# A two-layer encoder trunk: the memory norm's weights moved from the rows into the split, and the first transfers reordered

## The chip, the core and the metric

The kernel runs on one core of one Trainium2 chip. The metric is the device time of one execution in microseconds, the median of the runs. Engines: PE (TensorE, matrix products and transposes), DVE (VectorE), ACT (ScalarE), POOL (GpSimd) and SP (SyncE, which only issues transfers here). Each engine works through its own instructions in order and waits on semaphores for the others. Sixteen DMA engines move data between the chip's main memory and the on-chip buffer; matrix products go to a second on-chip memory, PSUM.

## The reference

Two layers of an encoder on 512 tokens of width 1024. Each layer normalizes x, projects it to queries, keys, values and a gate, attends over the tokens (dilated windows in layer 0, grouped queries in layer 1), attends over 256 memory tokens, gates, and projects back. The part that the change touches is the memory branch of layer 0:

```python
def rmsnorm(x, g):
    xf = x.astype(jnp.float32)
    y = xf * lax.rsqrt(jnp.mean(xf * xf, axis=-1, keepdims=True) + EPS)
    return (y * g.astype(jnp.float32)).astype(x.dtype)
...
    for i in range(DEPTH):
        h = rmsnorm(x, norm_g[i])
        mem_h = rmsnorm(mem, mem_norm_g[i])
...
    kv = jnp.einsum('bnd,de->bne', mem_h, w_kv).reshape(Bn, N, 2, MEM_HEADS, HEAD_DIM)
    k = rmsnorm(kv[:, :, 0], kn_g)
    v = kv[:, :, 1]
```

The norm's factor per row, rsqrt of the mean square, is applied later, to the keys' norm and to the values. What has to be in the memory rows before the product is the weight per column, mem_norm_g.

## The kernel before

Every float32 product is made of three matmuls on operands that are split in two: a high part rounded to float32r, and a low part, the rest. ACT makes the high part of a weight piece (line 323), DVE the low part (line 333). A group of matmuls has first the products that need only the high part of the weight (lines 176 and 177), then those with its low part (line 180). Weight pieces are 128x1024 float32, 512 KB, called W0, W1 and so on here in the order of their use.

The program is written out slot by slot by a small driver at build time. After each group of matmuls `W.advance` emits the next work on weights (low parts, high parts, loads) and `drv.tick` lets waiting generators take a step. Every engine then runs its instructions in the order in which they were emitted, whatever is ready.

The beginning goes as follows.

- Lines 1053 to 1075: the first transfers on SP's queue. The norm's weights for the memory as one row, the first half of memory rows 0 to 127, W0 and W1, rows 128 to 255 whole, the second half of rows 0 to 127, W2 and W3, x's norm weights broadcast to 128 partitions (`row_load`), W4 and W5, a small table, and the four 512 KB blocks of x with W6 and W7 between the second and the third.
- Lines 1115 to 1121: PE spreads the row of weights over 128 partitions by matmuls of a row of ones with it (`spread`).
- Lines 1128 to 1148: `times` multiplies a half of the memory rows (128x512) by that on DVE; `turn4` transposes it in four 128x128 pieces on PE; `place_m` splits the result into high and low parts of 128x512. `square` and `factor` make the norm's factor per row on ACT and POOL.
- Line 1189: the product for keys and values, `mem_kv`. The keys, K, take four groups: (u, b) is half u of the contraction with memory rows of block b. W0 and W1 serve u = 0, W2 and W3 u = 1. The values, V, follow with W4 to W7. `ahead(u, b)`, called within a group between its high and low matmuls, emits the splits of the blocks to come: `place_m(1, 0)` in group (0, 0), `place_m(0, 1)` and `place_m(1, 1)` in group (0, 1).
- Lines 1077 to 1095 and 1177: `prep`, which normalizes and transposes x, starts at slot 2 (PD), which is the tick after group (0, 1). In the tick after group (0, 1) it emits the squares of x's first block, x0, on ACT and its factor on POOL; in that after (1, 0) the squares of x1 and the multiplication of x0 on DVE (line 534); in that after (1, 1) the squares of x2, the multiplication of x1 and the transposes of x0 on PE (line 540); in that after V's first group those of x1.
- `W.advance` after group (0, 1) emits the high parts of W4 and W5, that after (1, 0) their low parts, that after (1, 1) the high parts of W6 and W7.

Of the kernel before, what the change touches and what calls it, by code (L numbers as in the profile page):

```python
# [10 lines left out]
F32 = mybir.dt.float32  # L11
F32R = mybir.dt.float32r
AF = mybir.ActivationFunctionType
ALU = mybir.AluOpType
# [14 lines left out]
DIRECT, DIRECT_B = (7,), (3, 4, 5, 6, 7)  # L29
LO_K, TURN_K, HI_V, LO_V = (4, 4), (8, 6), (1, 6), (9, 2)  # L30
PD = 2
EO = 2, 2, 1, 2, 2, 1
YB = {"m": (2, 2), "k": (1, 1, 1), 0: (1, 2, 1), 1: (1, 2, 1)}
Y = [3, 2, 2, 2, 3, 2, 2, 1, 1, 1]
# [9 lines left out]
KEEP_C = {0: 14, 3: 14, 4: 12}  # L44
KEEP = {"T2": 8, "T2b": 6, "O1": 6, "W1": 9, "W2": 10, "W2s": 9, "W1bs": 9, "W2c": 9, "W1b": 7, "W2b": 9, "W1o": 7}
# [86 lines left out]
def trunk_kernel(ctx: ExitStack, tc: tile.TileContext, x, mem, wall, norm_g, mem_norm_g, gcol,  # L132
                 qn_a, kn_a, qn_b, kn_b, ident_d, mask_d, tab_a, tab_b, out):
    nc = tc.nc
    V, A, G, T = nc.vector, nc.scalar, nc.gpsimd, nc.tensor

    pool = ctx.enter_context(tc.tile_pool(name="pool", bufs=1))
# [18 lines left out]
    def at(name="at"):  # L156
        return psum.tile([128, 512], F32, tag="at", name=name, bufs=4)
# [38 lines left out]
    class Weights:  # L196
# [63 lines left out]
            else:  # L260
                queue.dma_start(t, wall[d], **how)  # L261

        def dma(self, most=9):
            while self.allocs and self.live < KEEP_C.get(self.allocs[0][0][0], KEEP[self.allocs[0][2]]) and most:
                most -= 1
                key, d, _ = self.allocs.pop(0)
                self.live += 1
                self.tile[key] = m4(name="wl")
                self.load_at[key] = self.g
                if key[1][0] != "T":  # L270
                    self.at[key] = self.g
                self.load(nc.sync, self.tile[key], d)

        def ripe(self, at, key, force, n=None):
            return key in at and (force or self.g - at[key] >= (LEAD if n is None else n))
# [1 line left out]
        def sum(self, force=False, want=None):  # L277
# [33 lines left out]
                return True  # L311
            return False

        def hi(self, force=False):
            i = self.n_hi
            if i >= len(self.items) or not self.ripe(self.at, self.items[i], force, 1 if self.items[i][1] == "T1" and self.items[i][0] < T1_DMA else None):
                return False
            if i >= RING and self.last[i - RING] > self.g - (not force and self.items[i - RING][1] != "P"):
                return False
            self.n_hi += 1  # L320
            wh = pool.tile([128, 1024], F32R, tag="wh", name="wh", bufs=RING)
            wo = pool.tile([128, 1024], F32R, tag="wo", name="wo", bufs=RING)
            A.copy(wh, self.tile[self.items[i]])  # L323
            self.hi_at.append(self.g)
            self.op.append((wh, wo))
            return True

        def lo(self):
            i = self.n_lo
            self.n_lo += 1  # L330
            wh, wo = self.op[i]
            key = self.items[i]
            V.tensor_tensor(wo, self.tile[key], wh.bitcast(F32), ALU.subtract)  # L333
            self.lo_at[key] = self.g
            self.use(key)

# [30 lines left out]
    W = Weights()  # L367
# [129 lines left out]
    ropeA = tabs[:, 512:2048].rearrange("p (c b s e) -> p c b s e", c=2, b=4, s=6)  # L497
    half = pool.tile([128, 8], F32, name="half")
    rm = pool.tile([128, 6], F32, name="rm")
    ones = tabs[0:1, 0:128]  # L500
    V.memset(half, -0.5)
    V.memset(ones, 1.0)
    A.activation(small.tile([128, 1], F32, tag="sm1", name="warm"), half[:, 0:1], AF.Exp)

    class Act:
# [30 lines left out]
    def turn4(src, hi, lo, mid=None):  # L536

        p = at("xT")
        for k in range(4):
            T.transpose(p[:, k * 128:(k + 1) * 128], src[:, k * 128:(k + 1) * 128], ident)  # L540
# [513 lines left out]
    xt = [m4(name="x") for _ in range(4)]  # L1054
    rows = {}
    mt = [m4(name="m") for _ in range(2)]
    nc.scalar.dma_start(ident, ident_d)
    row0 = m4(name="row0")[0:1, :]
    nc.sync.dma_start(row0, mem_norm_g[0:1, :])
    nc.sync.dma_start(mt[0][:, 0:512], mem[0:128, 0:512])  # L1060
    W.dma(2)
    nc.sync.dma_start(mt[1], mem[128:256])
    nc.sync.dma_start(mt[0][:, 512:1024], mem[0:128, 512:1024])
    W.dma(2)
    row_load("x", norm_g[0:1, :])
    W.dma(2)
    tabA = s2(name="tabA")[:, 0:256].rearrange("p (b c d) -> p b c d", b=2, c=4)
    grA = s2(name="grA")[:, 0:192].rearrange("p (s c) -> p s c", s=6)
    nc.sync.dma_start(gc, gcol)
    for c in range(4):  # L1070
        nc.sync.dma_start(xt[c], xv[c])
        if c % 2 and c < 3:
            W.dma(2)
    H, H2 = {}, {}
    xb = [halves(t) for t in xt]
# [36 lines left out]
                            grA[:, None].to_broadcast([128, 4, 6, 32]), ALU.mult)  # L1112
            yield 1

    row = [at("row") for _ in range(2)]

    def spread(j, *cols):

        for c in cols:
            cs = slice(256 * c, 256 * c + 256)  # L1120
            T.matmul(row[j][:, cs], ones, row0[:, 512 * j + 256 * c:512 * j + 256 * c + 256], start=True, stop=True, skip_group_check=True)

    spread(0, 0, 1)
    mb, M = [halves(t) for t in mt], Act(NM)
    ss = [sm(2, "ss") for _ in range(2)]
    mg = {}

    def times(b, j):

        t = mg[b, j] = s2(name="mg")  # L1130
        V.tensor_tensor(t, mb[b][j], row[j], ALU.mult)

    def square(b, j):

        A.activation(s2(name="sq"), mb[b][j], AF.Square, scale=1.0 / 32.0, accum_out=ss[b][:, j:j + 1])

    def factor(b):

        e = sm(1, "mse")
        G.tensor_tensor(e, ss[b][:, 0:1], ss[b][:, 1:2], ALU.add)  # L1140
        r = rstd_of(e, 1)
        for k, by in enumerate((1.0, QS, 0.5)):
            G.tensor_scalar(rm[:, 2 * k + b:2 * k + b + 1], r, by, None, ALU.mult)

    def place_m(b, j, act=True, p=None):

        cs = slice(b * 128, (b + 1) * 128)
        split(M.block(0, j, cs), M.block(1, j, cs), p or turn4(mg[b, j], None, None), act)

    square(0, 0)  # L1150
    times(0, 0)
    spread(1, 0)
    p = turn4(mg[0, 0], None, None)
    spread(1, 1)
    W.hi(True)
    place_m(0, 0, False, p)
    W.hi(True)
    W.lo()
    times(1, 0)
    W.lo()  # L1160
    for b, j in ((1, 0), (0, 1), (1, 1)):
        square(b, j)
    for b in range(2):
        times(b, 1)
        factor(b)

    def ahead(u, b):

        if (u, b) == (0, 0):
            place_m(1, 0)  # L1170
            W.hi(True)
            W.hi(True)
        if (u, b) == (0, 1):
            place_m(0, 1)
            place_m(1, 1)

    drv.spawn(prep(), PD)
    drv.spawn(setup(), SET_AT)
# [611 lines left out]
```

## Time and profile before

| | us |
|---|---|
| median of 3 runs | 943.32 (943.01 to 944.55) |
| span of the profiled execution | 940.4 |
| PE busy | 932.0 |
| DVE busy | 799.6 |
| ACT busy | 691.6 |
| POOL busy | 348.4 |

The profiled execution is known by its span, from the first to the last instruction. Busy time is the time in which an engine works on an instruction; matmuls are pipelined, so a busy PE need not be at its peak. Rows of a timeline have start, duration, engine, line, operation, what is written from what, the count, and in brackets the idle time before with what ended it. Several instructions of one kind in a row are one row. SPq is SP's queue of transfers, whose rows are the issue, not the transfer. The mean granted clock of PE is 1.000.

### The profile page before, as it was taken

The page shows a single profiled execution, that of the slowest core. Times are in us where ns is not written, and L with a number is a line of the kernel's source. Part 1 is how long each engine was busy: PE and PEld are TensorE (multiplying, and loading weights), DVE is VectorE, ACT ScalarE, POOL GpSimd, SP SyncE. Part 2 cuts the span into 40 slices and gives each one's busy share as a digit, 9 for nine tenths or more (in the row PEclk, how much of TensorE's full clock was granted, in tenths as well). Part 3 has the DMA queues.
Part 4 walks back from the last instruction along what each step waited for, and adds up shares of the span by engine and source line. Part 5 has one row for each costly group of instructions (what it writes and reads, how often), then busy time and mean ns, then how long its engine had stood idle before and what let it go on. Part 6 is the DMA issues. An engine that isn't in the chain of part 4 may idle for free.

```text
span 940.4 us, 16301 instructions
## 1 busy us (share of the span) xinstructions
PE 932.0 (99%) x5500; PEld 819.4 (87%) x5500; DVE 799.6 (85%) x1443; ACT 691.6 (74%) x1720; POOL 348.4 (37%) x494
## 2 busy tenths in 40 slices
PE   8999999999999999999999999999999999999998
PEld 6889888888888888888889998888988999999886
DVE  6998776879888888889788999877998998689978
ACT  7775788677768686867675768537878887789773
POOL 3412425455554545463836111214252440110122
PEclk9999999999999999999999999999999999999999
DMA  9999937869787878696867979979985686785777
GB/s 346 387 259 324 316 93 189 278 133 262 155 251 146 261 155 267 158 268 136 242 177 190 269 202 249 291 239 317 270 201 118 171 240 167 198 225 121 200 159 179
DMA packets 89285, 207.15 MB, mean 220 GB/s; under 512 B 25201, under 2 KB 34417, under 8 KB 89202
## 3 DMA queue, kind: packets, MB, share of 16 engines
q1 hardware_dynamic: 68674, 140.51, 43.5%
q0 software_dynamic: 19520, 63.97, 36.8%
q10 hardware_dynamic: 1008, 1.64, 0.5%
q8 instruction: 43, 0.70, 0.3%
q14 instruction: 40, 0.33, 0.1%
HBM read 158.31 MB, written 11.08 MB: 180 GB/s over the span
## 4 chain that ended last, share of the span: by engine, by line
PE 95%; DVE 2%; ACT 1%; DMA 1%; issue 0%; SPq 0%; DVEq 0%; ACTq 0%
PE pj L177 25%; PE pj L176 25%; PE pj L180 25%; PE qT L645 3%; PE sa L1305 2%; PE oo L1413 2%; PE pt L1392 1%; PE ptb L1619 1%; PE sa L1301 1%; PE xT L540 1%; PE ob L180 1%; PE ob L177 1%; PE ob L176 1%; PE sb L171 1%; PE sb L170 1%; PE sb L172 1%
## 5 line engine op out<-in xcount | busy, mean ns | idle before, releaser
L333 DVE TENSOR_TENSOR wo<-wl,wh 128x1024 fp32r<-128x1024 f32 x258 | 316.3, 1232 | 6.9 <-ACT wh L323 6.7
L323 ACT CAST wh<-wl 128x1024 fp32r<-128x1024 f32 x258 | 272.1, 1061 | 31.0 <-PE pj L177 17.4
L176 PE MATMUL pj<-wh,hS 128*128 128x512 f32 (+1 forms) x416 | 154.4, 380 | 0.0
L177 PE MATMUL pj<-wh,hS 128*128 128x512 f32 (+1 forms) x416 | 149.0, 367 | 0.0
L176 PE MATMUL pj<-wh,h 128*128 128x512 f32 (+1 forms) x312 | 115.3, 378 | 0.0
L177 PE MATMUL pj<-wh,h 128*128 128x512 f32 (+1 forms) x312 | 111.7, 367 | 0.0
L488 POOL TENSOR_TENSOR rstd<-mse,half 128x4 f32<-128x4 f32 (+2 forms) x98 | 103.4, 1056 | 8.2
L180 PE MATMUL pj<-wo,hS 128*128 128x512 f32 (+1 forms) x416 | 99.5, 366 | 0.0
L177 PEld LDWEIGHTS pj<-wh,hS 128*128 128x128 f32 x416 | 78.7, 189 | 11.2
L176 PEld LDWEIGHTS pj<-wh,hS 128*128 128x128 f32 x416 | 78.6, 189 | 11.1 <-DVE sn L420 0.2
L487 POOL TENSOR_SCALAR mse<-hss 128x4 f32<-128x4 f32 (+1 forms) x88 | 47.8, 543 | 101.9 <-ACT junk L633 94.2
L180 PEld LDWEIGHTS pj<-wo,hS 128*128 128x128 f32 x416 | 72.5, 189 | 13.1
L633 ACT ACTIVATE junk<-sn 128x128 f32<-128x128 f32 x264 | 79.4, 311 | 2.7 <-DVE sn L411 2.6
L398 ACT COPY sn<-pj 128x512 f32<-128x512 f32 x122 | 67.1, 588 | 17.8 <-PE pj L180 17.0
L1249 POOL TENSOR_TENSOR ta<-sn,tabs 128x128 f32<-128x128 f32 (+1 forms) x64 | 35.8, 566 | 119.0 <-DVE sn L638 91.8
L180 PE MATMUL pj<-wo,h 128*128 128x512 f32 (+1 forms) x312 | 74.5, 365 | 0.0
L307 POOL DMA_DIRECT2D wl<-wl x34 | 30.2, 897 | 113.3 <-DVE wo L333 73.3
L261 POOL DMA_DIRECT2D wl<-in_wall_dram x40 | 38.0, 966 | 80.4 <-DMA wl<-in_wall_dram 41.0
L177 PEld LDWEIGHTS pj<-wh,h 128*128 128x128 f32 x312 | 59.0, 189 | 8.4
L176 PEld LDWEIGHTS pj<-wh,h 128*128 128x128 f32 x312 | 59.0, 189 | 8.2
L420 DVE TENSOR_TENSOR sn<-pj,sn 128x512 f32<-128x512 f32 x89 | 60.8, 684 | 5.7 <-PE pj L180 5.3
L180 PEld LDWEIGHTS pj<-wo,h 128*128 128x128 f32 x312 | 54.3, 189 | 9.7
(290 smaller groups left out, 2367.2 us busy)
## 6 DMA issues: line engine op xcount, KB each, us to landing
wl<-in_wall_dram SPq DMA_DIRECT2D x224, 512.0 KB, 7.4
wl<-wl POOLq DMA_DIRECT2D x68, 512.0 KB, 5.5
wl<-in_wall_dram POOLq DMA_DIRECT2D x44, 512.0 KB, 8.5
od<-o SPq DMA_DIRECT2D x11, 256.0 KB, 5.4
og<-od SPq DMA_DIRECT2D x10, 256.0 KB, 9.5
x<-in_x_dram SPq DMA_DIRECT2D x4, 512.0 KB, 9.1
v0d<-sn SPq DMA_DIRECT2D x8, 256.0 KB, 8.5
acc<-in_x_dram POOLq DMA_DIRECT2D x8, 256.0 KB, 6.2
```

The source lines that it names most:

```text
L176: T.matmul(o, a, b, start=start, stop=False, skip_group_check=True)
L177: T.matmul(o, c, d, start=False, stop=False, skip_group_check=True)
L180: T.matmul(o, a, b, start=False, stop=stop, skip_group_check=True)
L261: queue.dma_start(t, wall[d], **how)
L323: A.copy(wh, self.tile[self.items[i]])
L333: V.tensor_tensor(wo, self.tile[key], wh.bitcast(F32), ALU.subtract)
L398: A.copy(t, b)
L420: V.tensor_tensor(t, b, t, ALU.subtract if q == "12" else ALU.add)
L487: G.tensor_scalar(e, ss, EPS, None, ALU.add)
L488: G.tensor_tensor(r, e, half[:, 0:n], ALU.pow)
L633: A.activation(jk, p[:, j * 128:(j + 1) * 128], AF.Square, scale=by, accum_out=ss[:, j:j + 1])
L1249: G.tensor_tensor(ta[:, 0:n], xn[:, 0:n, 0:32], ropeA[:, 0, b, s0:s0 + n], ALU.mult)
```

## The change

The memory rows are transposed as they come. The norm's weights come as a table of 16 rows by 128, are transposed on PE to one column per 128 features (`gmc`), and are applied in the split: the high part is the transposed piece times its column, rounded; the low part is the piece times its column less the high part. As each 128x128 piece has its own column, a block's split is four plus four operations in place of one plus one. The row's matmuls and the four multiplications of rows go.

The first two weight pieces come in two halves each, and their high and low parts are made by halves. Memory rows come in four 256 KB pieces between the weight pieces. x's norm weights come after W4 and W5. While the first transfers run, PE makes 12 matmuls on zeros. `place_m(1, 1)` with its squares and its factor moves from group (0, 1) to group (1, 0); the squares of block 0 move into group (0, 1). For the first three groups no more than 10 weight pieces are held.

```diff
+FINE, WARM, START_KEEP = 2, 12, 10
...
-        def dma(self, most=9):
-            while self.allocs and self.live < KEEP_C.get(self.allocs[0][0][0], KEEP[self.allocs[0][2]]) and most:
+        def dma(self, most=9, then=None):
+            while self.allocs and self.live < (START_KEEP if self.g < 3 else 99) and self.live < KEEP_C.get(self.allocs[0][0][0], KEEP[self.allocs[0][2]]) and most:
...
-                self.load(nc.sync, self.tile[key], d)
+                if len(self.load_at) > FINE:
+                    self.load(nc.sync, self.tile[key], d)
+                    continue
+                for c in (slice(0, 512), slice(512, 1024)):
+                    nc.sync.dma_start(self.tile[key][:, c], wall[d][:, c])
+                    if then:
+                        then()
+                        then = None
...
+        def cuts(self, i):
+            return (slice(0, 512), slice(512, 1024)) if i < FINE else (slice(0, 1024),)
...
-            A.copy(wh, self.tile[self.items[i]])
+            for c in self.cuts(i):
+                A.copy(wh[:, c], self.tile[self.items[i]][:, c])
...
-            V.tensor_tensor(wo, self.tile[key], wh.bitcast(F32), ALU.subtract)
+            for c in self.cuts(i):
+                V.tensor_tensor(wo[:, c], self.tile[key][:, c], wh[:, c].bitcast(F32), ALU.subtract)
...
-    ones = tabs[0:1, 0:128]
+    zero = tabs[:, 0:128]
+    V.memset(zero, 0.0)
     V.memset(half, -0.5)
-    V.memset(ones, 1.0)
...
-    nc.scalar.dma_start(ident, ident_d)
-    row0 = m4(name="row0")[0:1, :]
-    nc.sync.dma_start(row0, mem_norm_g[0:1, :])
-    nc.sync.dma_start(mt[0][:, 0:512], mem[0:128, 0:512])
-    W.dma(2)
-    nc.sync.dma_start(mt[1], mem[128:256])
-    nc.sync.dma_start(mt[0][:, 512:1024], mem[0:128, 512:1024])
-    W.dma(2)
+
+    def mem_load(b, j):
+
+        nc.sync.dma_start(mt[b][:, j * 512:(j + 1) * 512], mem[b * 128:(b + 1) * 128, j * 512:(j + 1) * 512])
+
+    W.dma(2, lambda: mem_load(0, 0))
+    mem_load(1, 0)
+    W.dma(1)
+    mem_load(0, 1)
+    W.dma(1)
+    mem_load(1, 1)
+    W.dma(2)
     row_load("x", norm_g[0:1, :])
-    W.dma(2)
...
+    gm = s2(name="gm")[0:16, 0:128]
+    gmc = pool.tile([128, 16], F32, name="gmc")
+    nc.scalar.dma_start(gm, mem_norm_g.rearrange("l (k p) -> (l k) p", p=128))
+    nc.scalar.dma_start(ident, ident_d)
+    idle = at("idle")
+    for _ in range(WARM):
+        T.matmul(idle[:, 0:128], zero, zero, start=True, stop=True, skip_group_check=True)
+    gt = at("gt")[:, 0:16]
+    T.transpose(gt, gm, ident[0:16, 0:16])
+    V.tensor_copy(gmc, gt)
...
-    def place_m(b, j, act=True, p=None):
-
-        cs = slice(b * 128, (b + 1) * 128)
-        split(M.block(0, j, cs), M.block(1, j, cs), p or turn4(mg[b, j], None, None), act)
...
+    def place_m(b, j, act=True):
+
+        p = turn4(mb[b][j], None, None)
+        for k in range(4):
+            kk, cs = 4 * j + k, slice(b * 128, (b + 1) * 128)
+            hi, lo, g = M.part[0][kk][:, cs], M.part[1][kk][:, cs], gmc[:, kk:kk + 1]
+            if act:
+                A.activation(hi, p[:, k], AF.Copy, scale=g)
+            else:
+                V.tensor_scalar(hi, p[:, k], g, None, ALU.mult)
+            V.scalar_tensor_tensor(lo, p[:, k], g, hi.bitcast(F32), ALU.mult, ALU.subtract)
+
     W.hi(True)
-    place_m(0, 0, False, p)
     W.hi(True)
+    place_m(0, 0, False)
     W.lo()
-    times(1, 0)
     W.lo()
-    for b, j in ((1, 0), (0, 1), (1, 1)):
-        square(b, j)
-    for b in range(2):
-        times(b, 1)
-        factor(b)
...
         if (u, b) == (0, 1):
             place_m(0, 1)
+            square(0, 0)
+            square(0, 1)
+            factor(0)
+        if (u, b) == (1, 0):
             place_m(1, 1)
+            square(1, 0)
+            square(1, 1)
+            factor(1)
```

More of the change, by code (lines that the diff above doesn't have):

```diff
@@ L1071, in trunk_kernel @@
         nc.sync.dma_start(xt[c], xv[c])
-        if c % 2 and c < 3:
+        if c == 1:
             W.dma(2)
@@ L1113, in setup @@
             yield 1
[L1115 to L1123, printed above, removed]
+    gm = s2(name="gm")[0:16, 0:128]
[8 more added lines that the diff above has]
+    V.tensor_copy(gmc, gt)
     mb, M = [halves(t) for t in mt], Act(NM)
     ss = [sm(2, "ss") for _ in range(2)]
[L1126 to L1131, printed above, removed]
     def square(b, j):
@@ L1143, in factor @@
             G.tensor_scalar(rm[:, 2 * k + b:2 * k + b + 1], r, by, None, ALU.mult)
-    def place_m(b, j, act=True, p=None):
-        cs = slice(b * 128, (b + 1) * 128)
-        split(M.block(0, j, cs), M.block(1, j, cs), p or turn4(mg[b, j], None, None), act)
[L1150 to L1154, printed above, removed]
+    def place_m(b, j, act=True):
[8 more added lines that the diff above has]
+            V.scalar_tensor_tensor(lo, p[:, k], g, hi.bitcast(F32), ALU.mult, ALU.subtract)
     W.hi(True)
-    place_m(0, 0, False, p)
     W.hi(True)
+    place_m(0, 0, False)
     W.lo()
-    times(1, 0)
     W.lo()
-    for b, j in ((1, 0), (0, 1), (1, 1)):
-        square(b, j)
-    for b in range(2):
-        times(b, 1)
-        factor(b)
     def ahead(u, b):
```

## The prediction

> **What bounds the kernel now.** I read the page first, then busy time by stretches, then the timelines of each engine over the first 45 us, because the diff touches nothing else.
>
> ```profile
> span 940.4 us, 16301 instructions
> PE 932.0 (99%) x5500; PEld 819.4 (87%) x5500; DVE 799.6 (85%) x1443; ACT 691.6 (74%) x1720; POOL 348.4 (37%) x494
> 24.00:48.00 24.00, 24.00 (x120) 20.10 (x119) 22.46 (x30) 18.19 (x39) 9.49 (x15) 1.00 1.03 388
> 900.00:940.40 40.40, 35.74 (x165) 29.31 (x163) 33.39 (x47) 20.64 (x32) 11.54 (x13) 0.99 0.74 157
> PE pmt L772 <- DVE pmT L778: 0.7, 1, 0.7
> ```
>
> The stretch rows give length, then busy time of PE, PEld, DVE, ACT and POOL, the granted clock, the DMA share and GB/s. PE is busy for all 24.00 of 24.00 us after the start, and the longest PE wait after that is the 0.7 us of the last row. So PE's queue behind 24 us is rigid: what moves its work at 24 us moves the end by as much. The question is only when the first rows of x, x0, get transposed on PE, since from there on PE never pauses. The span is 940.4 us and the median of the runs is 943.32, so about 2.9 us lie outside the span; I make the sum in the span and add the difference to the median.
>
> ```profile
> 2.24 2.89 PE L1121 MATMUL row<-row,tabs 1*128 1x256 f32 x6 [2.24 <-DMA row<-in_mem_norm_g_dram]
> 7.28 0.80 PE L176 MATMUL pj<-wh,act 128*128 128x512 f32 x1
> 8.30 0.63 PE L176 MATMUL pj<-wh,act 128*128 128x512 f32 x1
> 8.73 0.63 PE L177 MATMUL pj<-wh,act 128*128 128x512 f32 x1
> 10.95 0.50 PE L177 MATMUL pj<-wh,act 128*128 128x512 f32 x1
> 19.77 0.39 PE L176 MATMUL pj<-wh,act 128*128 128x512 f32 x1
> 20.00 0.39 PE L177 MATMUL pj<-wh,act 128*128 128x512 f32 x1
> 21.59 1.07 PE L180 MATMUL pj<-wo,act 128*128 128x512 f32 x4
> 22.77 1.06 PE L540 MATMUL xT<-ident,x 128*128 128x128 f32 x8
> 26.43 1.04 PE L540 MATMUL xT<-ident,x 128*128 128x128 f32 x8
> ```
>
> Columns: start, duration, engine, line, what. The K product starts at 7.28; its matmuls follow each other by 0.43 us (8.30 to 8.73) until 10.95, later by 0.23 (19.77 to 20.00). The fourth and last group of K, which I call K(1,1), runs from 19.77 to 22.66. At 22.77 PE transposes x0. Is that time PE's own, or x0's?
>
> ```profile
> 0.73 0.34 SPq L1059 DMA_DIRECT2D row<-in_mem_norm_g_dram  x1
> 1.13 0.37 SPq L1060 DMA_DIRECT2D m<-in_mem_dram  x1
> 9.70 0.99 SPq L1071 DMA_DIRECT2D x<-in_x_dram  x2
> DMA to landing us min/median/max: 8.7/8.7/8.7
> 16.74 2.01 ACT L323 CAST wh<-wl 128x1024 fp32r<-128x1024 f32 x2
> 18.63 0.64 ACT L527 ACTIVATE sq<-x 128x512 f32<-128x512 f32 x1
> 19.87 0.63 ACT L527 ACTIVATE sq<-x 128x512 f32<-128x512 f32 x1
> 20.05 0.19 POOL L529 TENSOR_TENSOR mse<-ss 128x1 f32<-128x1 f32 x1 [2.89 <-ACT sq L527]
> 20.63 0.57 POOL L488 TENSOR_TENSOR rstd<-mse,half 128x1 f32<-128x1 f32 x1
> 17.83 2.36 DVE L333 TENSOR_TENSOR wo<-wl,wh 128x1024 fp32r<-128x1024 f32 x2
> 21.23 1.44 DVE L534 SCALAR_TENSOR_TENSOR x<-x,rstd,row 128x512 f32<-128x512 f32 x2 [1.04 <-POOL rstd L488]
> ```
>
> Both, to a tenth. The landing row is that of the first x transfer alone: issued at 9.70, landed at 18.4. ACT squares it from 18.63 (x1's squares follow at 19.87), POOL makes rstd until 21.20, DVE multiplies until 22.67, PE transposes at 22.77. PE's last K group ended at 22.66. Two chains end together, and the change shortens PE's. I call the start of x0's squares s; before, s = 18.63 and the transposes come at s + 4.14.
>
> **Does x0 land sooner?** Hardly.
>
> ```profile
> 2.50:5.00 2.50, 2.50 (x6) 1.53 (x5) 0.69 (x1) 0.72 (x2) 0.00 (x0) 1.00 0.99 324
> 17.50:20.00 2.50, 2.50 (x12) 2.05 (x11) 2.35 (x3) 2.50 (x7) 0.00 (x0) 1.00 1.02 410
> 933.00:934.00 1.00, 1.00 (x7) 0.81 (x6) 1.00 (x3) 0.00 (x0) 0.00 (x0) 1.00 1.00 379
> ```
>
> The DMA engines are full from 2.5 us on, and the diff puts the same bytes ahead of x0: 1 MB of memory rows, six weight pieces, the broadcast row (moved behind pieces five and six). Removing the row issue at 0.73 lets the first large transfer start 0.4 us earlier, at 0.73 in place of 1.13. Against that, 1.57 MB now move in rows of 2 KB in place of 4 KB; the only stretch of 2 KB rows alone (output, 933 to 934) runs at 379 GB/s against 410 for 4 KB rows, which gives 0.3 us. So x0 lands at 18.0 to 18.4.
>
> **The change, part by part.** The row multiplications (four on DVE) and the four row matmuls go. The zeros: the six records of three 256-column float32 matmuls take 2.89 us, 0.96 each; twelve of 128 columns are half as long, 5.8 us at that pace and less if the clock opens, so from about 1.0 to about 6.0. PE is in order, so the first transposes of memory rows stand behind them; the first of them landed 2.8 after its issue at 1.13, at about 4, and its place is the same now, so it is the zeros that end last. The little gain matrix (on ACT's queue, ahead of ident), its transpose and copy fall before 6.5.
>
> ```profile
> DMA to landing us min/median/max: 2.8/2.8/2.8
> 175.45 0.63 ACT L1260 ACTIVATE ks<-qT,gk 128x128 f32<-128x128 f32 x2 [1.28 <-PE qT L645]
> 166.48 0.35 DVE L1261 TENSOR_SCALAR ks<-qT,gk 128x128 f32<-128x128 f32 x1 [0.97 <-ACT ks L1260]
> 166.75 0.68 DVE L420 TENSOR_TENSOR sn<-pj,sn 128x512 f32<-128x512 f32 x1
> 11.00 0.62 ACT L1135 ACTIVATE sq<-m 128x512 f32<-128x512 f32 x1
> 11.52 0.19 ACT L1135 ACTIVATION_READ_ACCUMULATOR sq<-m 128x1 f32 x1
> 11.18 0.40 POOL L1140 TENSOR_TENSOR mse<-ss 128x1 f32<-128x1 f32 x1 [10.74 <-ACT sq L1135]
> 12.66 0.82 POOL L1143 TENSOR_SCALAR rm<-rstd 128x1 f32<-128x1 f32 x3
> 13.44 0.19 POOL L1140 TENSOR_TENSOR mse<-ss 128x1 f32<-128x1 f32 x1
> 16.38 0.78 POOL L1143 TENSOR_SCALAR rm<-rstd 128x1 f32<-128x1 f32 x3
> 22.17 0.92 POOL L488 TENSOR_TENSOR rstd<-mse,half 128x1 f32<-128x1 f32 x1
> ```
>
> The first of these rows is the landing of the first memory rows. The new split works on 128x128 tiles out of PSUM with a scale per partition. ACT has that very form at L1260: two take 0.63, so 0.26 each after the first of 0.37, and four take 1.15. On DVE the tensor-by-scalar form takes 0.35 with the next instruction 0.27 later, so 0.08 overlaps. The subtraction with scale at 128x128 from PSUM is not in the trace: between 0.27 (that form) and 0.6 (the pitch of 128x512 at L333's rate, half of a piece's 1.14). I take 0.28, nearest to the same size and source, and keep both ends. Four of them take 1.1 us.
>
> Now the queue of each engine. The first block's split on DVE is eight small operations, each second one waiting for the one before it: about 2.6 us, from 6.5 to 9.2; the two low parts of the weights (2.28 us, the 2.36 at 17.83 less the overlap) until 11.6; then the second block's four, two more weight pieces and the third block's four, until about 16. PE follows DVE: K(0,0) runs from 7.0 to 12.1, K(0,1) to 15.2, K(1,0) from about 15.4 to 18.4. ACT has the third block's four high parts at 14.4 to 15.5, two squares (0.62 each) to 16.75 and the two casts W4 and W5 (2.01 at 16.74) to 18.65. So s is the later of landing (18.0 to 18.4) and ACT (17.5 to 18.9): I take 18.5, against 18.63.
>
> Then comes the added wait. The fourth block, rows 128 to 255, second half, is now split inside group (1,0), and the step that emits x0's squares is the tick after group (0,1), thus ahead of it. On ACT the fourth block's high parts therefore stand behind x0's squares, which wait for x0's landing. On DVE, behind its four low parts stand the low parts of W4 and W5 (emitted after group (1,0)), which before ran at 17.83 while everybody waited for x0, and behind those x0's multiplication. The sum, from s:
>
> - ACT is free 1.24 after s (18.63 to 19.87); the first high part, and 0.40 later (the lead of ACT over DVE at L1260 and L1261) the first low part: s + 1.64
> - four low parts by 0.28: s + 2.76
> - W4 and W5, 2.28: s + 5.04
> - x0's multiplication, 1.44, and 0.10 to PE: s + 6.58
>
> With s = 18.5 the transposes of x0 start at 25.08 in place of 22.77: 2.3 us later. K(1,1) runs from about 20.5 to 23.2 and does not set it. W2 and W3 keep slack, since ready by 15.
>
> What is late next: x1. Behind the fourth block ACT has its two squares (1.24) and then x1's (1.24), so x1's end at s + 4.9. On POOL the fourth block's factor comes first: 11.18 to 13.48 is 2.3 us, 13.44 to 17.16 is 3.7; from s + 3.7 it ends at s + 6.0 to s + 7.4. x0's rstd took 1.15 (20.05 to 21.20) and x1's came 1.89 behind it (23.09, the last row). So x1's multiplication starts at s + 7.2 to s + 9.3 and its transposes are ready at s + 8.7 to s + 10.8, middle 28.2. PE arrives at 25.08 + 3.66 = 28.74 (22.77 to 26.43). Nothing is added in the middle, up to 0.5 at the upper end. x2 and x3 have over 1 us of slack in the timeline and move along. The weight loads that START_KEEP holds back are behind x3 in SP's queue anyway; nothing else is queued on SP there, so I cost them at nothing; were they late, the s_chunk of v0 at 37 us would show PE waiting.
>
> Sum: x0 +2.3, x1 0 to +0.5, small tiles -0.1 to +0.5 (DVE 0.6 in place of 0.28 would add 1.3, at the far bound), s -0.4 to +0.4. The forecast is 943.3 + 2.3 = 945.6, its own range 945.1 to 947.0. A measurement here tells about 0.2%, 1.9 us, from no change, so the forecast lies just beyond it.
>
> **The clock.** The rows at 8.30 and 19.77 show half and full pace. The first eight matmuls of K lose about 0.2 each, 1.6 us. The Trainium skill (TensorE: Matmul & The Clock Gate, Part 1) says that the array starts at half clock and that about 3.4 us of sustained activity, an interval and not a count, opens it. The trace agrees: full pace comes about 3.7 us after 7.28. By that rule alone the zeros would bring 1.6 us, and the sum would be 941.7.
>
> **Rivals.** (1) The early gain reaches the end: PE gets through K faster and x0 does not hold it. Without the queue on ACT, K(1,1) would end at 18.4 + 2.7 = 21.1, that is 1.6 earlier, 941.7; more if the zeros are shorter. The case decides if x0's chain of 4.14 can start by 17, thus if x0 lands 1.4 us sooner. The 324 GB/s of the start against 410 speak for some room (0.5 us in that stretch), the order of ACT's queue against it. This is the case on the other side; chance 0.10. (2) s comes early, at about 17.0, since DMA reaches 410 GB/s at once and the zeros end by 4.5; the queue is as I say but starts sooner: 17.0 + 6.58 = 23.6, +0.8, 944.1. Below s = 18.1 it is no measurable loss. Chance 0.18. (3) PE idles from 18.4 to 20.5 and from 23.2 to 25.1, and the clock falls back: twelve matmuls of the next group at 0.43 in place of 0.23 are 2.4 us, 948.0. It decides if an idle stretch grows to about the 3.7 us that opening took; I have 2.1 and 1.9. Chance 0.08. The Trainium skill (same page and part) lets the clock fall after one idle window of about 3.4 us; no row here shows a fall. (4) The change does not do what it says: the zeros last until 6.8 at half pace and delay the first block, ACT gets free at 19.4, s + 6.58 = 26.0, +3.2, 946.5. Chance 0.04.
>
> **The numbers.** Forecast 0.60. Of it 0.82 lies beyond 0.2% (0.49), the rest within; rivals 3 and 4 add 0.11 slower, less 0.01: 0.59. Same: 0.11 + rival 2's 0.18 + half of rival 1 (0.05) and 0.02 = 0.36. Faster: the other half, 0.05. The range 942.6 to 947.6 leaves out rival 1 and rival 3 and little of the forecast.
>
> **What would show it.** Right: ACT's x0 squares near 18.5, the fourth block's four scale-copies directly behind them, the two weight low parts on DVE between those and x0's multiplication, x0's transposes on PE near 25, PE idle in two pieces before. Wrong: the fourth block split before 18, or x0 landed before 17, or the x transposes at or before 22.8; also PE idle at a later step, which I have nowhere.

## The result, and the profile after

The changed kernel takes 952.69 us (median of 4 runs, 951.79 to 954.24) beside 943.86 for the kernel before, measured with it: 8.8 us slower by the medians, a ratio on record of 1.010, interval 1.009 to 1.011. The direction was forecast, the size was 2.3, and the time lies outside the range, 942.6 to 947.6. The page of the changed kernel, and its busy time over the stretch that the prediction looked at:

```profile
span 951.2 us, 16365 instructions
PE 939.2 (99%) x5517; PEld 821.6 (86%) x5517; DVE 800.8 (84%) x1457; ACT 693.8 (73%) x1731; POOL 346.5 (36%) x494
```

```profile
24.00:48.00 24.00, 21.72 (x100) 16.74 (x101) 18.77 (x27) 20.00 (x54) 13.05 (x24) 0.93 0.98 386
```

The engines have the same work as before to within a per cent, but PE is busy for 21.72 of these 24 us in place of all. PE's timeline says where (lines have moved: x's transposes are now L553, K's matmuls L177, L178 and, with the low weights, L181):

```profile
8.09 0.47 PE L177 MATMUL pj<-wh,act 128*128 128x512 f32 x1 [0.54 <-DVE act L1165]
25.11 0.51 PE L177 MATMUL pj<-wh,act 128*128 128x512 f32 x1 [2.33 <-ACT act L1163]
28.52 1.91 PE L181 MATMUL pj<-wo,act 128*128 128x512 f32 x4
31.46 1.09 PE L553 MATMUL xT<-ident,x 128*128 128x128 f32 x8 [1.03 <-DVE x L547]
35.16 1.03 PE L553 MATMUL xT<-ident,x 128*128 128x128 f32 x8
```

x0's transposes start at 31.46 (22.77 before, 25.08 forecast), and they still wait 1.03 us for x0. x1's follow 3.70 later without a wait, as before. K(1,1) waited 2.33 us for the fourth block. So the delay of 8.7 us is all there at x0. Now ACT and DVE, the two engines that split the blocks:

```profile
11.29 0.37 ACT L1163 ACTIVATE act<-xT,gmc 128x128 fp32r<-128x128 f32 x1 [2.27 <-PE xT L553]
12.96 0.37 ACT L1163 ACTIVATE act<-xT,gmc 128x128 fp32r<-128x128 f32 x1 [1.30 <-DVE act L1166]
16.69 0.37 ACT L1163 ACTIVATE act<-xT,gmc 128x128 fp32r<-128x128 f32 x1
18.53 0.37 ACT L1163 ACTIVATE act<-xT,gmc 128x128 fp32r<-128x128 f32 x1 [1.47 <-DVE act L1166]
19.32 0.37 ACT L1163 ACTIVATE act<-xT,gmc 128x128 fp32r<-128x128 f32 x1 [0.42 <-DVE act L1166]
20.10 0.37 ACT L1163 ACTIVATE act<-xT,gmc 128x128 fp32r<-128x128 f32 x1 [0.42 <-DVE act L1166]
20.37 0.62 ACT L1146 ACTIVATE sq<-m 128x512 f32<-128x512 f32 x1
21.59 1.98 ACT L335 CAST wh<-wl 128x1024 fp32r<-128x1024 f32 x2
23.48 0.63 ACT L540 ACTIVATE sq<-x 128x512 f32<-128x512 f32 x1
24.71 0.35 ACT L1163 ACTIVATE act<-xT,gmc 128x128 fp32r<-128x128 f32 x1
```

```profile
15.87 2.36 DVE L346 TENSOR_TENSOR wo<-wl,wh 128x1024 fp32r<-128x1024 f32 x2 [0.58 <-ACT wh L335]
18.15 0.34 DVE L1166 SCALAR_TENSOR_TENSOR act<-xT,gmc,act 128x128 fp32r<-128x128 f32 x1
18.93 0.35 DVE L1166 SCALAR_TENSOR_TENSOR act<-xT,gmc,act 128x128 fp32r<-128x128 f32 x1 [0.44 <-ACT act L1163]
19.71 0.35 DVE L1166 SCALAR_TENSOR_TENSOR act<-xT,gmc,act 128x128 fp32r<-128x128 f32 x1 [0.44 <-ACT act L1163]
25.10 0.35 DVE L1166 SCALAR_TENSOR_TENSOR act<-xT,gmc,act 128x128 fp32r<-128x128 f32 x1 [4.25 <-ACT act L1163]
27.72 2.35 DVE L346 TENSOR_TENSOR wo<-wl,wh 128x1024 fp32r<-128x1024 f32 x2
29.99 1.41 DVE L547 SCALAR_TENSOR_TENSOR x<-x,rstd,row 128x512 f32<-128x512 f32 x2
```

```profile
ACT act L1163 <- DVE act L1166: 5.7, 9, 1.5
```

Read the brackets crosswise. DVE waits 0.44 for ACT, which is plain: the low part of a piece needs its high part. But ACT waits 0.42 for DVE before each next piece (the last row: 9 waits, 5.7 us in all, the longest 1.5), and a high part needs no low part. The wait is in the program: in the trace each of these copies of ACT waits on a semaphore that DVE counts up. The two take turns: 19.32, 19.71, 20.10, a piece every 0.785 us where each engine alone needs some 0.27. And the waiting hands DVE's queue on to ACT: at 16.69 ACT makes a first piece, then stands until 18.53, because the first low part stands behind two weight pieces on DVE (15.87 to 18.15). From 20.10 on ACT has no gap until x0's squares at 23.48.

### The profile page after: what moved, and what is told of

Same layout as the page of the kernel before. It is cut to its first block, busy times and chain, and to the rows that moved or that the text cites. A ratio compares the mean times of both kernels' runs of the same rounds, so it can differ in the third digit from the quotient of the medians.

```text
span 951.2 us, 16365 instructions
## 1 busy us (share of the span) xinstructions
PE 939.2 (99%) x5517; PEld 821.6 (86%) x5517; DVE 800.8 (84%) x1457; ACT 693.8 (73%) x1731; POOL 346.5 (36%) x494
## 4 chain that ended last, share of the span: by engine, by line
PE 90%; DVE 3%; DMA 2%; ACT 2%; POOL 1%; issue 1%; SPq 0%; DVEq 0%; POOLq 0%; ACTq 0%
PE pj L177 24%; PE pj L178 24%; PE pj L181 24%; PE qT L658 3%; DMA wl<-in_wall_dram 2%; PE sa L1319 2%; PE oo L1427 2%; PE ptb L1633 1%; PE pt L1406 1%; PE sa L1315 1%; DVE wo L346 1%; DMA row<-in_norm_g_dram 1%; PE ob L181 1%; PE ob L178 1%; PE ob L177 1%; PE sb L171 1%
## 5 line engine op out<-in xcount | busy, mean ns | idle before, releaser
L346 DVE TENSOR_TENSOR wo<-wl,wh 128x1024 fp32r<-128x1024 f32 (+1 forms) x260 | 316.6, 1225 | 7.2 <-ACT wh L335 7.2
L335 ACT CAST wh<-wl 128x1024 fp32r<-128x1024 f32 (+1 forms) x260 | 271.7, 1052 | 32.1 <-PE pj L178 15.5
L177 PE MATMUL pj<-wh,hS 128*128 128x512 f32 (+1 forms) x416 | 154.6, 380 | 0.1
L178 PE MATMUL pj<-wh,hS 128*128 128x512 f32 (+1 forms) x416 | 149.1, 367 | 0.0
L177 PE MATMUL pj<-wh,h 128*128 128x512 f32 (+1 forms) x312 | 115.3, 378 | 0.0
L178 PE MATMUL pj<-wh,h 128*128 128x512 f32 (+1 forms) x312 | 111.8, 367 | 0.0
L181 PE MATMUL pj<-wo,hS 128*128 128x512 f32 (+1 forms) x416 | 99.8, 367 | 0.0
L177 PEld LDWEIGHTS pj<-wh,hS 128*128 128x128 f32 x416 | 78.6, 189 | 11.6 <-ACT sn L411 0.5
L178 PEld LDWEIGHTS pj<-wh,hS 128*128 128x128 f32 x416 | 78.6, 189 | 11.3
L181 PEld LDWEIGHTS pj<-wo,hS 128*128 128x128 f32 x416 | 72.4, 189 | 13.3
L181 PE MATMUL pj<-wo,h 128*128 128x512 f32 (+1 forms) x312 | 74.7, 366 | 0.0
L178 PEld LDWEIGHTS pj<-wh,h 128*128 128x128 f32 x312 | 58.9, 189 | 8.5
L177 PEld LDWEIGHTS pj<-wh,h 128*128 128x128 f32 x312 | 58.9, 189 | 8.2
L181 PEld LDWEIGHTS pj<-wo,h 128*128 128x128 f32 x312 | 54.3, 189 | 9.9
```

Source lines behind the costliest of these rows:

```text
L177: T.matmul(o, a, b, start=start, stop=False, skip_group_check=True)
L178: T.matmul(o, c, d, start=False, stop=False, skip_group_check=True)
L181: T.matmul(o, a, b, start=False, stop=stop, skip_group_check=True)
L335: A.copy(wh[:, c], self.tile[self.items[i]][:, c])
L346: V.tensor_tensor(wo[:, c], self.tile[key][:, c], wh[:, c].bitcast(F32), ALU.subtract)
```

## Experiments

Theory A: the turns are forced, because the four pieces of a block lie in one PSUM bank and ACT and DVE are not let into one bank at the same time; they hold up ACT's queue and make most of the delay. A', a rival of it, has the turns from the alternation of the instructions whatever the bank. B puts the delay on the order of ACT's queue (the fourth block behind x0's squares), C on the zeros. Times are medians, with the ratio to the kernel before measured beside them (its medians are 942.6 to 943.9); the ratios are as recorded and differ from those of the medians by up to 0.0008. "x0" is the start of x0's transposes in the profiled execution.

| kernel | us | ratio, 95% | x0 |
|---|---|---|---|
| after | 952.69 | 1.0102 (1.0090 to 1.0114) | 31.46 |
| e1 two passes | 948.47 | 1.0062 (1.0047 to 1.0077) | 26.61 |
| e2 block back | 954.75 | 1.0131 (1.0116 to 1.0146) | 32.63 |
| e3 one multiplication | 950.06 | 1.0077 (1.0062 to 1.0093) | 26.18 |
| e4 no zeros | 954.38 | 1.0125 (1.0108 to 1.0142) | 32.14 |
| e5 two banks | 947.51 | 1.0049 (1.0033 to 1.0066) | 27.66 |
| e6 before, in pieces | 948.07 | 1.0060 (1.0045 to 1.0075) | 27.18 |
| e7 before, block late | 944.03 | 1.0015 (1.0006 to 1.0025) | 24.63 |
| e8 in order | 944.71 | 1.0023 (1.0014 to 1.0032) | 24.09 |
| f1 before, x0 first | 943.97 | 1.0015 (1.0006 to 1.0025) | 23.66 |
| f2 early K | 947.60 | 1.0050 (1.0036 to 1.0065) | 23.11 |
| f3 early K, filled | 945.44 | 1.0022 (1.0012 to 1.0032) | 21.01 |
| f4 as f3, x0 late | 945.70 | 1.0030 (1.0020 to 1.0040) | 24.13 |

**e1: all four high parts first, then all four low parts.** Nothing else moves.

```diff
+                V.scalar_tensor_tensor(lo, p[:, k], g, hi.bitcast(F32), ALU.mult, ALU.subtract)
+        for k in range(4) if act else ():
...
             V.scalar_tensor_tensor(lo, p[:, k], g, hi.bitcast(F32), ALU.mult, ALU.subtract)
```

> Edit: in the changed kernel's split, ACT makes the four high parts of a block first and DVE the four low parts after, in place of piece by piece. Theory A (turns at one PSUM tile: ACT's next high part waits for DVE's low part of the piece before, 0.79 us a piece): a block holds ACT for 1.15 us in place of about 3.5, x0's squares start near 19.2 in place of 23.48, x0's transposes near 26.6 in place of 31.46, and the time falls by about 4.9 us to 947.8. Theory B (only the order of ACT's queue, the fourth block behind x0's squares, costs): the order is unchanged, so the time stays within 0.5 us of the changed kernel's 952.7.

ACT's, PE's and DVE's timelines of e1 for the fourth block:

```profile
20.67 1.14 ACT L1163 ACTIVATE act<-xT,gmc 128x128 fp32r<-128x128 f32 x4
```

```profile
21.09 0.50 PE L177 MATMUL pj<-wh,act 128*128 128x512 f32 x1 [0.94 <-ACT act L1163]
```

```profile
21.84 1.13 DVE L1170 SCALAR_TENSOR_TENSOR act<-xT,gmc,act 128x128 fp32r<-128x128 f32 x4 [4.23 <-ACT act L1163]
```

The prices of the prediction, 1.15 and 1.1 for four, come back as 1.14 and 1.13, x0's squares start at 19.43, and x0 gains 4.85 us. Yet DVE starts only when ACT is done with the bank (21.84), where the first high part was ready by 21.09, when PE's product starts with it. x0's place is as Theory A expected, the time 0.7 us above it.

**e5: the same order of instructions as after, but the pieces alternate between two banks.**

```diff
-        p = turn4(mb[b][j], None, None)
+        two = [at("xT") for _ in range(2)]
+        ps = [two[k % 2][:, k // 2 * 128:k // 2 * 128 + 128] for k in range(4)]
```

> Edit: in the changed kernel's split the four transposes of a block go alternately into two PSUM tiles of a bank each; the order of instructions on every engine stays as it was, piece by piece. Theory A (ACT and DVE take turns because both read the same PSUM bank): ACT's next piece lies in the other bank and does not wait for DVE's last, so two pieces take what one took, 0.8 us; a block holds ACT about 1.6 us in place of 3.1, x0's squares start near 21 in place of 23.48, its transposes near 27.7 in place of 31.46, and the time falls by about 3.8 us to 949. Theory A' (the turns come from the order of emission, whatever the bank): nothing changes, 952.7.

ACT and DVE of e5, the fourth block:

```profile
22.23 0.61 ACT L1166 ACTIVATE act<-xT,gmc 128x128 fp32r<-128x128 f32 x2
23.00 0.63 ACT L1166 ACTIVATE act<-xT,gmc 128x128 fp32r<-128x128 f32 x2 [0.17 <-DVE act L1169]
```

```profile
22.61 0.61 DVE L1169 SCALAR_TENSOR_TENSOR act<-xT,gmc,act 128x128 fp32r<-128x128 f32 x2 [4.24 <-ACT act L1166]
23.40 0.61 DVE L1169 SCALAR_TENSOR_TENSOR act<-xT,gmc,act 128x128 fp32r<-128x128 f32 x2 [0.18 <-ACT act L1166]
```

The block takes 1.8 us in place of 3.1, and 3.8 of x0's 8.7 us go, with the instructions in the same order. x0 comes where Theory A expected it, and A' is refuted: what counts is whether neighbouring pieces share a bank. (A tile in PSUM is one whole bank in these kernels, so the runs don't tell a rule by bank from one by tile.) The Trainium skill (PSUM — Partial Sum Buffer, PSUM bank collisions raise a hardware error) says that two engines must not touch one bank (in the same quarter of the partitions) at once, reads against reads of ACT and DVE included, that the hardware does not arbitrate, and that the compiler adds a dependency between their instructions. The trace agrees: within a bank the engines alternate at 0.39 us, between two banks they overlap.

**e2: after, with the fourth block and the factor back in group (0,1), still piece by piece.**

```diff
             place_m(0, 1)
+            place_m(1, 1)
...
-        if (u, b) == (1, 0):
-            place_m(1, 1)
```

> Edit: the fourth block's split with its squares and factor goes back into group (0,1), ahead of x0's squares; the split stays piece by piece. Theory B (queue order): x0's chain is free of the fourth block, its transposes come 4.1 us after its squares, the time falls by about 3.8 us to 948.9. Theory A (turns at the PSUM tile): the fourth block takes its 3 us ahead of x0's squares in place of behind them, with two more squares, so the squares start near 28, the transposes near 32, and the time is 953 to 954.

x0 moved to 32.63 and the time to 954.75, near what Theory A expected. With the turns in place it is no help to have the block ahead: its 3.1 us then stand before x0's squares, at 27.17. B alone is refuted.

**e7: the kernel before with only that block moved to (1,0)**, split in one piece as before.

```diff
             place_m(0, 1)
+        if (u, b) == (1, 0):
             place_m(1, 1)
```

> Edit: the kernel before with nothing changed but that the fourth memory block is split inside group (1,0) in place of (0,1), thus behind x0's squares on ACT. Theory B (queue order, as forecast): the low parts of W4 and W5 come behind it and ahead of x0's multiplication, the chain from x0's squares grows from 4.1 to 6.3 us, x0's transposes come near 25, 2.2 us slower than before: 945.2. If the order costs nothing: 943.0.

```profile
24.63 1.06 PE L540 MATMUL xT<-ident,x 128*128 128x128 f32 x8 [0.80 <-issue]
```

From s = 18.26 to 24.63 are 6.37 us (4.14 before): as long as the prediction's chain of 6.58, although the block is one operation on each engine there and the first two terms differ (1.98 and 0.61 in place of 1.64 and 1.12). It costs 1.9 at x0 and 1.4 in the time.

**e6: the kernel before with blocks two to four split piece by piece** (four plain casts and four subtractions).

```diff
+        for k in range(4):
+            A.copy(hi, p[:, k])
+            V.tensor_tensor(lo, p[:, k], hi.bitcast(F32), ALU.subtract)
```

> Edit: the kernel before with nothing changed but that the splits of three of the four memory blocks are made in four pieces, high on ACT and low on DVE in turn, in place of one high and one low part of 128x512. Theory A alone: each block takes about 3.1 us, x0's squares move from 18.6 to about 25.5 and its transposes from 22.8 to about 29.6: 6.8 us slower than before, 949.8. If the turns cost only the additional instructions (three more of 0.2 us on each engine and block), about 1 us.

PE's timeline of e6 and its clock (20 to 27 and 27 to 30 us):

```profile
27.18 1.94 PE L540 MATMUL xT<-ident,x 128*128 128x128 f32 x8 [3.48 <-issue]
```

```profile
20.00:27.00 7.00, 3.69 (x17) 2.71 (x15) 4.60 (x7) 6.29 (x22) 2.12 (x6) 0.94 1.03 411
27.00:30.00 3.00, 2.82 (x11) 2.66 (x12) 2.02 (x6) 3.00 (x6) 2.43 (x5) 0.50 1.02 410
```

The turns alone, with nothing else of the change, cost 4.4 at x0: 0.625 us a piece. The expectation had 6.8, since it took the 0.785 of the pieces with scale. After 3.48 us of idleness the granted clock is at half, and x1 comes 6.35 behind x0 in place of 3.66: another 2.7, the prediction's rival 3 (2.4) in another kernel.

**e3: DVE multiplies a whole block out of PSUM by the broadcast column, and the copy is split.**

```diff
+        t = s2(name="mg").rearrange("p (k t) -> p k t", k=4)
+        V.tensor_tensor(t, p, gmc[:, 4 * j:4 * j + 4, None].to_broadcast([128, 4, 128]), ALU.mult)
```

> Edit: DVE multiplies a whole transposed block by its columns of weights into the on-chip buffer in one 128x512 operation, and the split is one high and one low operation of 128x512 from there. Theory A: no turns are left, s falls to about 20.6, x0's transposes to about 27, the time by 4.5 us to 948.2, though the fourth block still stands behind x0's squares. Theory B: order unchanged, within 0.7 us of 952.7.

x0 comes at 26.18, close to e1's 26.61, and the intervals of the two times overlap. The time, 950.06, is 1.9 above the expectation although x0 came 0.8 ahead of it; the profiled execution was the fastest of the four, 948.26. The multiplication takes 0.69 on DVE, a high and a low part then come from on-chip memory outside PSUM, and nobody takes turns.

**e4: no zeros.** `WARM = 0` in place of 12.

> Edit: no matmuls on zeros, all else as changed. Theory C (the zeros hold the first transposes until 6.9 while the rows land at 4.3): the first block is split about 2.4 us earlier, everything behind it up to x0's squares too, 950.5. Theory D (the zeros buy the full clock and K would run at half pace without them): K's first groups are paced by DVE, not by PE, so at most 0.5 us is lost by this; if PE's pace counts, the time is 953 or more.

```profile
6.38 0.26 PE L1139 MATMUL gt<-ident,gm 16*128 16x16 f32 x1 [6.38 <-DMA ident<-in_ident_dram]
8.22 0.76 PE L177 MATMUL pj<-wh,act 128*128 128x512 f32 x1 [0.54 <-DVE act L1165]
8.78 0.63 PE L178 MATMUL pj<-wh,act 128*128 128x512 f32 x1
```

C is refuted. The wait for ident ends at 6.38 and would hold the first transposes in any case; without zeros K starts no earlier (8.22) and runs at 0.43 a matmul. x0 comes 0.7 later than with them, a little more than the 0.5 that theory D allowed; the time is 954.38, and its interval overlaps that of the changed kernel.

**e8: two passes, and block, squares and factors back in their places of before.**

```diff
             place_m(0, 1)
-            square(0, 0)
-            square(0, 1)
-            factor(0)
-        if (u, b) == (1, 0):
             place_m(1, 1)
```

> Edit: the changed kernel with both causes taken out: ACT's four high parts first and DVE's four low parts after, the fourth block back in group (0,1), and the squares of the memory rows in ACT's idle stretches before 16 us. Theories A and B together explain all but 0.7 us: x0's squares near 19.3, its transposes near 23.5, the time 943.7, within 0.2% of before. If the transfers in pieces or the zeros cost something of their own, 945 or more; if the early gain of PE reaches the end after all, 941.5.

PE and POOL of e8:

```profile
24.09 1.09 PE L553 MATMUL xT<-ident,x 128*128 128x128 f32 x8 [1.42 <-DVE x L547]
```

```profile
19.11 2.37 POOL L1154 TENSOR_SCALAR rm<-rstd 128x1 f32<-128x1 f32 x3
21.44 0.19 POOL L542 TENSOR_TENSOR mse<-ss 128x1 f32<-128x1 f32 x1
```

From e1 to e8 x0 gains 2.5 us, so this is what the order of the queues cost beside the turns. Of the 1.3 that are left against before, 0.8 is s (19.42; two blocks now take ACT 2.17 us, the two casts took 1.08), and 0.6 is POOL, where the second block's factor ends at 21.44 in front of x0's. K(1,1) ends at 22.66, exactly as before: the early gain is not there. The gains of e1 and e8 and these 1.3 add up to the 8.7. The time, 944.71, is 1.0 above the expectation, x0 0.6 behind it.

**f1: is PE's chain really the other one that binds?** The kernel before, with x0's transfer ahead of W4 and W5 and its squares and multiplication emitted earlier.

```diff
     row_load("x", norm_g[0:1, :])
+    nc.sync.dma_start(xt[0], xv[0])
     W.dma(2)
```

> The kernel before with x0's transfer moved ahead of the weight pieces W4 and W5, x0's squares emitted in group (0,1) and its multiplication in group (1,0). In the kernel before two chains end together, x0's at 22.77 and K(1,1)'s at 22.66. If both bind, as the theory has it, taking x0's chain away alone moves x0's transposes by about 0.1 us at most, to 22.6 to 22.8, and the time by -0.3 to +0.3 from 942.6. The rival, that x0's chain alone set the end and K(1,1) followed it, gives transposes near 21 and a time near 941.

ACT's first cast and PE's view of x0 in f1:

```profile
7.48 1.05 ACT L323 CAST wh<-wl 128x1024 fp32r<-128x1024 f32 x1 [2.62 <-DMA wl<-in_wall_dram]
```

```profile
23.66 1.03 PE L540 MATMUL xT<-ident,x 128*128 128x128 f32 x8
```

x0 was ready by 21.9 and PE reached it at 23.66 without a wait, so in f1 PE's own queue set it. But W0 came 1.3 us later here than before, and K with it; both figures of the expectation missed, and whether the edit or the execution delayed W0 is open. So f1 does not show where PE's chain alone would have put x0 in the kernel before.

**f2, f3, f4: can K be early, and does it help?** f2 is e8 with eight matmuls on zeros in place of 12 (the 24 of its expectation are the trace's records, two for each), ident first, the first memory transposes ahead of the gains', one multiplication for the first block, and x0 early as in f1. f3 adds four zeros behind the gains' transpose and takes the factors apart (block 0's ahead of x0's on POOL, block 1's behind). f4 is f3 with x0 in its place of before.

```diff
     V.tensor_copy(gmc, gt)
+    for _ in range(FILL):
+        T.matmul(idle[:, 0:128], zero, zero, start=True, stop=True, skip_group_check=True)
```

> The kernel after with the turns taken away (high parts of a block first, then low parts), the fourth block and the memory rows' squares back in their places of before, eight zeros in place of 24, ident issued first on ACT's queue, the first memory transposes ahead of the gains' transposes, and x0 early as in the other kernel of this call. If K's start and the turns are all that kept the early gain from K(1,1), K starts at about 7.2 at nearly full pace, K(1,1) ends at about 21.2, x0's transposes start at 21.2 to 21.5 and the time is about 941.2 (941 to 942). The rival, that K(1,1) waits for the wait of its block on DVE whatever K's start, keeps K(1,1)'s end at 22.5 and the time at 942.6 to 943.7.

> The kernel f2 with its two faults mended: four more zeros on PE behind the gains' transpose, so that PE does not idle the 1.54 us in which the clock fell (granted 0.60 from 7.4 to 11.1), and the factor of block 0 on POOL before x0's, that of block 1 behind x0's. If the early gain can reach the end, K starts at about 7.4 at full pace, its first group ends by about 11.5 in place of 12.66 before, K(1,1) ends at 21.3 to 21.8, x0's transposes follow at once (its chain was ready at 22.2 in f2, so 22.2 at the earliest by that), x1's at about 25.9, and the time is 942.0 to 942.5. If the gain is lost again in the groups between, on the low parts of the weights and the casts, K(1,1) ends at 22.5 or later and the time is 942.7 or more.

> The same with x0's transfer and squares in their places of before. K as in the other kernel of this call; x0's squares come at 19.4 as in the kernel in which all was put back in order, POOL is free for them, so rstd is ready 1.0 us sooner than there, the multiplication starts near 21.7 and x0's transposes near 23.2: +0.4 at x0, a time of 943.0 to 943.4 whatever K does, since x0's chain sets the end.

f2, PE's timeline, and the clock behind the zeros (5.8 to 7.4, 7.4 to 11.1) and behind the wait for x1 (from 29.48):

```profile
4.62 0.67 PE L553 MATMUL xT<-ident,m 128*128 128x128 f32 x4
7.40 0.47 PE L177 MATMUL pj<-wh,act 128*128 128x512 f32 x1 [1.54 <-DVE act L167]
29.48 1.09 PE L553 MATMUL xT<-ident,x 128*128 128x128 f32 x8 [2.58 <-DVE x L547]
```

```profile
5.80:7.40 1.60, 0.06 (x1) 0.03 (x1) 1.40 (x4) 1.12 (x2) 0.00 (x0) 1.00 1.05 384
7.40:11.10 3.70, 3.54 (x8) 2.45 (x9) 2.99 (x5) 1.98 (x6) 0.00 (x0) 0.60 1.01 375
29.48:33.00 3.52, 3.52 (x20) 3.05 (x21) 2.50 (x4) 3.24 (x13) 2.10 (x5) 1.00 1.01 403
```

f3, the same rows, and at the boundary of the layers PE's and DVE's waits:

```profile
6.87 0.47 PE L177 MATMUL pj<-wh,act 128*128 128x512 f32 x1 [0.46 <-DVE act L167]
21.01 1.04 PE L553 MATMUL xT<-ident,x 128*128 128x128 f32 x8
25.37 1.09 PE L553 MATMUL xT<-ident,x 128*128 128x128 f32 x8 [0.56 <-DVE x L547]
32.23 1.06 PE L553 MATMUL xT<-ident,x 128*128 128x128 f32 x8 [0.26 <-DMA wl<-in_wall_dram]
```

```profile
PE pj L177 <- DVE acc L433: 1.0, 1, 1.0
```

```profile
DVE yf L879 <- DMA og<-od: 3.2, 1, 3.2
```

f2 missed for two reasons of its own: PE idled 1.54 us before K and the clock was at half from about 8 to 11 us, and POOL's factors stood in front of x1's (2.58 of idleness). f3 mends the first and most of the second, and it is the one kernel that has the early gain: x0 at 21.01, 1.76 sooner than before. It still is slower than before, 945.44, where 942.0 to 942.5 was expected. Against before it is 1.06 ahead at x1, for which PE waits 0.56 (block 1's factor still stands before x1's on POOL), 0.54 at x2, where PE waits 0.26 for the landing of a weight piece, and 0.08 at the queries (50.80 for 50.88). Then it falls behind: by 1.1 at 524 us, by 3.4 at 615. In between DVE waits 3.2 us for rows of attention that come back through memory (`og`; 0.5 before), and PE waits for DVE. f4 has x0 at 24.13 (23.2 expected: its squares came at 19.87, and K ran at half clock until about 10); 945.70. No kernel here beats the one before.

## Why the prediction was wrong

**The bound, and the two chains.** Right in the place: what happened to x0 is most of the result (8.7 us; 10.9 at 786 us of the profiled executions, 8.8 between the medians). "What moves its work at 24 us moves the end by as much" holds only in part. In the profiled executions e7's 1.8 and e6's 7.1 us stand within 0.1 from 51 us to 786. In every other kernel PE falls further behind on the way, by 1.0 (e8) to 2.9 us (e2) at 786 us, and by more in f2 and f3; f1 is among them, 0.89 at x0 and 2.75 at 786 us, although it is made from the kernel before. For gains it fails: f3's 1.76 is gone by 51 us. The prediction had the full DMA engines in its rows and asked only what they do to x0; in f3 PE meets the landing of a weight at x2. What took the last 0.4 of the 1.76, between 45 and 51 us, was not followed.

**The step that failed** is "so 0.26 each after the first of 0.37, and four take 1.15", with "0.40 later (the lead of ACT over DVE at L1260 and L1261)". The price of an operation was right, 1.14 for four in e1. That both engines work on a block with a lead was wrong: in one bank they take turns, 3.1 us a block. The 0.40 was not a lead but half a turn. By terms, s came at 23.48 in place of 18.5: the third block started 2.3 late, because ACT had waited through the second, and took 3.7 in place of 1.15. From s, the chain was 7.98 in place of 6.58: four low parts took 2.62 (25.10 to 27.72) in place of 1.12, the other terms were 1.62 for 1.64, 2.27 for 2.28 and 1.47 for 1.54. The sum, 5.0 and 1.4, is the 6.4 between 31.46 and 25.08. The kernel before could have warned. Its waits at L1261, in total and how often:

```profile
  ACT ks L1260: 17.7, 15
```

DVE waited there 15 times, 17.7 us in all, for ACT. Most of that is the wait of both for PE's transposes; the turn is the last 0.40 of a wait (ACT at 175.45, DVE at 175.85). The two lines write different parts of `ks` and need nothing of each other; they only read neighbouring pieces of one PSUM tile.

**What held.** x0 landed at 18.6, a little late (10.34 plus 8.3; 18.0 to 18.4 forecast), and bound nothing. The order of the queues was right, row for row: the fourth block behind x0's squares, the low parts of W4 and W5 before x0's multiplication; e7 shows its price alone, 1.9 at x0, and e1 less e8 puts it at 2.5, where the prediction had 2.3 in all. The first block took 2.6 us on DVE, x1 does not wait.

**What else missed.** K began at 8.09, not 7.0. ident, now second on ACT's queue, lands 5.1 us after its issue (2.4 before). Rival 1, the early gain, did not come: in this form K(1,1) ends with or after its time of before until ident comes first and PE is kept busy (f3), and then it is given back. Rival 3 happened in small: PE idled 2.33 us at 22.8, short of the 3.7 that the rival asked for, and from about 27.1 K(1,1) ran at half clock (1.91 for the four at 28.52, 1.07 before), hidden behind x0's wait of 1.03. In the part on the clock, "full pace comes about 3.7 us after 7.28" leaves out that PE had worked almost without a gap since 2.24, so the opening there took some 8.7 us and does not bear out 3.4. And the 2.9 us outside the span compare a median with another execution: in the runs that list both, time and span differ by 1.8. The sum does not hang on it.

**Open.** In the profiled execution the 8.7 at x0 are 9.5 at 51 us, 10.1 at 524, 10.5 at 615 and 10.9 at 786, while the medians differ by 8.8. So between kernels x0's place and the time agree only to some 2 us, in e3, f2 and f3 to about 4. Two places are known and not explained: every kernel made from the changed one loses 0.3 us between 615 and 665 us, those made from the kernel before do not; and what decides when the `og` rows land (DVE waits 0.5 to 3.5 us for them from kernel to kernel) was not tried.

## What to carry to other kernels

Before cutting a PSUM tile into pieces for two engines, ask which bank the pieces lie in: in one bank the engines took turns here, at 0.785 us a piece where each alone needs 0.27, and each also inherited the other's queue. Put one engine through the whole tile first, or lay alternate pieces in different banks. And an engine's early start may be a loan: before counting it, follow it past the next points where the engine waits for others or for data (f3's 1.76 us were 0.08 at 51).

## What the runs showed of the hardware

- Two engines that alternate on one bank: 0.785 us a pair of 128x128 operations with scale (0.37 and 0.35 long), 0.625 for plain ones (0.27 and 0.29); on two banks 0.39.
- The clock fell after 1.54 us of idleness in f2 (its four transposes at 4.62 took 0.67, where e4's without zeros took 1.11; then K's matmuls at 0.43, granted 0.60), after 3.48 in e6, and about 2 us after PE had gone on from 2.33 of idleness in the changed kernel and 1.97 in e5. It stayed up after 0.46 in f3, 1.42 in e8, 1.57 in e1 and 2.58 in f2 (granted 1.00 from 29.48). So the length of one idle stretch does not decide it alone; what does was not tried. The Trainium skill (TensorE: Matmul & The Clock Gate, Part 1: The HAM clock gate (the "warmup" mystery)) speaks of an idle window of about 3.4 us; e6 agrees, f2 fell sooner, and here the measurement decides.
- The clock's opening differed between two kernels with the same beginning on PE: eight matmuls on zeros from 1.04 (3.78 us in both) opened it by 4.62 in f2, and in f4 full pace came at about 10.
- Three tiny POOL operations (128x1) took 0.82 us at 17.08 in e8 and 2.37 at 19.11, while DVE was making low parts of weights; that DVE is the cause was not tried.
